# The first pass over two convolution maps at once, row by row

## The chip, the cores and the metric

The kernel runs on one core of a Trainium2 chip. A core has a matrix engine (TensorE, in the profile PE, with its weight loads as PEld), VectorE (DVE), ScalarE (ACT), GpSimd (POOL) and SyncE (SP), each with an instruction queue of its own that runs in order; they wait for one another through semaphores. Weights come from memory by DMA, which SP, ACT and POOL issue. Matmuls write to PSUM, which has eight banks of 512 f32 columns here; everything else stands in SBUF. The metric is the time of one execution on the device in microseconds (us): the median of several runs. Beside it stands one execution with the profiler on.

## The reference

One layer of a decoder trunk for 256 tokens and 16 learned meta tokens in front of them (272 columns in all), width 2048, float32:

```python
u = rms_norm(h, g_pre_mix)
proj = u @ w_in
z_pool, v_conv, g_conv, gate_a, gate_b = split(proj)     # 1024, 1024, 1024, 2048, 2048
y_a = causal_multiscale_pool(z_pool, w_pool_grp, pool_scale) @ w_pool_out
a = v_conv * sigmoid(g_conv)
c = depthwise_causal_conv(a, w_dw) + b_dw                # 31 taps
y_b = silu(layer_norm(c, conv_ln_g, conv_ln_b)) @ w_conv_out
m = sigmoid(gate_a) * y_a + sigmoid(gate_b) * y_b
h = h + rms_norm(m @ w_o, g_post_mix)
f = square(relu(rms_norm(h, g_pre_mlp) @ w_up)) @ w_down
out = (h + rms_norm(f, g_post_mlp))[16:]
```

The change lies in the first lines: the normed input, and the first 256 columns each of `v_conv` and `g_conv`, the two maps whose gated product goes into the convolution.

## The kernel before

**Precision.** Each f32 operand is cut in two parts that the fast matmul type holds: `hi`, a cast on ACT, and `lo`, the rest, a subtraction on DVE. A product of the first projection is three matmuls (`mm3`, L422): weight hi by input hi, weight hi by input lo, weight lo by input hi. Each has 128 weight columns as its stationary side and 272 columns of `u` as its moving side.

**Weights.** `stream` lists all weight chunks of 1 MB in order of use. `open_chunk` (L246) issues a chunk's DMA into one of three `raw` rooms and leaves its casts as pieces to be done; `fetch` opens and splits up to two chunks ahead. A whole chunk is split in one piece: a cast of 128x2048 (L250) and a subtraction of 128x2048 (L253). For the first pass the pieces are rows: one row is 128 input channels, here by 256 columns. The hi and lo parts of chunks rotate through three rooms each.

**The input.** `u` holds, for each of 16 blocks `k` of 128 channels, hi and lo of the input, transposed, with channels on partitions, and times `g_pre_mix`. `x_tile(k)` transposes two blocks of x on TensorE into PSUM (L370); ACT takes the hi part (L371), DVE the lo part (L372). `meta_tokens` does the same for the 16 meta tokens, by 16 transposes of 16 rows. The RMS factor isn't applied to `u`: it depends on the token alone, so it is applied to the products later. `sq_tile` (L380) sums squares on ACT in twelve pieces of 512 columns into `ssq`; `scale_roots` makes the factor and three diagonal tiles from it; `scale_rows` (L412) spreads it over all partitions by f32 matmuls with a tile of ones, and copies it into `rb`. `evac_v` and `evac_g` multiply by `rb`.

**The first passes.** Pass v0 makes 256 columns of `v_conv` in two accumulators. Its loop runs over k with a lead of four: four x tiles and four rows of weights are issued before the first product, then each pair of rows is followed on TensorE by two more x tiles. Pass g0 (256 columns of `g_conv`) and the later ones go through `project`, which takes whole chunks and, after each half chunk, lets `drain` issue some of the `pending` work: the squares, the roots, `after_first` (L412 and the evacuation of v0), `tap_columns`, and then the taps of the convolution. In the profile v0 begins at 7.97 us, g0 at 23.52, and the second pair, v1, at 35.36.

**Before the first product** SP issues the meta tokens and x, ACT `g_pre_mix` and more of x; the framework gives the transfers of SP and ACT eight completion semaphores in turn, so that a ninth one waits for the landing of the first. `keep_warm` (L343) issues transposes of the identity that nobody reads. SP's order is: meta, one half of x's first 512 columns, weight rows, x's third 512 columns, weight rows of the second chunk, x's last columns.

**Later stages** (pool, gates, output projections, the two MLP products, the last norm) aren't touched. A planner orders the last stages by costs and due times; it has no part in what is changed.

Of the kernel before, what the change touches and what calls it, by code (L numbers as in the profile page):

```python
# [8 lines left out]
F32 = mybir.dt.float32  # L9
F32R = mybir.dt.float32r  # L10
AF = mybir.ActivationFunctionType
# [3 lines left out]
P = 128  # L15
CK = 4
CW = 512
# [83 lines left out]
def hybrid_block(ctx: ExitStack, tc: tile.TileContext, ins: dict, out: bass.AP):  # L101
# [83 lines left out]
    G0 = PW + 2 * CC  # L185
    HALF = (2 * CK, CW // 2)
    HALF_CW = CW // 2
    stream = []
# [21 lines left out]
    FIRST = KD // HALF[0]  # L210
    opened = []
    at = {"n": 0, "parts": 0}

# [16 lines left out]
        shift = (place - 1 - 3 * KEYS.index(key)) % 4 * LINE  # L230
        return room[:, shift:shift + CK * CW]

    def open_chunk(first=((2, nc.sync),) * 4):
# [7 lines left out]
        pieces = rows if n < FIRST + 1 else 1  # L241
        k = rows // pieces
        i = 0
        for n_, queue in first if n < FIRST else ((rows, nc.sync),):
            sl = slice(i, i + n_)
            queue.dma_start(raw[:, sl, :], src[:, sl, :])  # L246
            i += n_

        def high(sl):
            nc.scalar.copy(hi[:, sl, :], raw[:, sl, :])  # L250

        def low(sl):
            nc.vector.tensor_sub(lo[:, sl, :], raw[:, sl, :], f32(hi[:, sl, :]))  # L253

        def piece(i):
            def f():
                sl = slice(i * k, (i + 1) * k)
                high(sl)
                low(sl)
            return f  # L260
        opened.append((hi, lo, [piece(i) for i in range(pieces)], flat))

    def split_pieces(c):
        while opened[c][2]:
            opened[c][2].pop(0)()
# [18 lines left out]
    def warm_up(func):  # L284

        nc.scalar.activation(warm, ones[:, 0:1], func)
# [28 lines left out]
    def col(name, k):  # L315
        return vecs[:, cols[name] + k:cols[name] + k + 1]

    def load_x(queue, b, ts=slice(0, NT)):
        sl = slice(b * CW, (b + 1) * CW)
        queue.dma_start(x_in[:, ts, sl], xv[:, ts, sl])  # L320


    nc.sync.dma_start(m_in, meta)
    pre_rows = load_rows(nc.scalar, "g_pre_mix")
    for t, queue in enumerate((nc.sync, nc.scalar)):
        load_x(queue, 0, slice(t, t + 1))
    open_chunk(((1, nc.scalar), (1, nc.sync), (2, nc.sync), (2, nc.sync), (2, nc.sync)))
    load_x(nc.scalar, 1)
# [8 lines left out]
    warm_up(AF.Sqrt)  # L337

    idle = misc_tile("idle")

    def keep_warm(n):
        for _ in range(n):
            nc.tensor.transpose(idle[:, :P], ident, ident)  # L343

    keep_warm(8)

# [1 line left out]

    def meta_tokens():

        pt = acc_tile("xm")[:, :KD * M].rearrange("p (k m) -> p k m", k=KD)
        for k in range(KD):
            nc.tensor.transpose(pt[:, k, :], m_in[:, k * P:(k + 1) * P], ident[:M, :M])
# [4 lines left out]
        nc.scalar.copy(u[:, :, 0, :M], mg)  # L360
        nc.vector.tensor_sub(u[:, :, 1, :M], mg, f32(u[:, :, 0, :M]))

    meta_tokens()
    keep_warm(4)

    def x_tile(k):
        pt = acc_tile(f"xt_{k}")[:, :T]
        sl = slice(k * P, (k + 1) * P)
        for t in range(NT):
            nc.tensor.transpose(pt[:, t * P:(t + 1) * P], x_in[:, t, sl], ident)  # L370
        nc.scalar.activation(u[:, k, 0, M:], pt, AF.Copy, scale=col("g_pre_mix", k))  # L371
        nc.vector.scalar_tensor_tensor(  # L372
            u[:, k, 1, M:], pt, col("g_pre_mix", k), f32(u[:, k, 0, M:]),
            op0=ALU.mult, op1=ALU.subtract)

    def sq_tile(b, t):
        sl = slice(b * CW, (b + 1) * CW)
        junk = tmp.tile([P, CW], F32, tag="junk", bufs=1, name=f"sqx_{b}_{t}")
        src, n = (x_in[:, t, sl], P) if t < NT else (m_in[:, sl], M)
        nc.scalar.activation(junk[:n, :], src, AF.Square, accum_out=ssq[:n, t, b:b + 1])  # L380

    def rsqrt(r, q, var):

# [6 lines left out]
    rb = const.tile([P, L], F32, name="rb")  # L390
    sc = {}

    def scale_roots():
# [23 lines left out]
    def mm3(acc, hi, lo, act, k, cs, first, last):  # L417


        off = act.shape[3] - acc.shape[1]  # L420
        for n, (w, a) in enumerate(((hi, 0), (hi, 1), (lo, 0))):
            nc.tensor.matmul(acc, w[:, k[0], cs], act[:, k[1], a, off:],  # L422
                             start=first and n == 0, stop=last and n == 2)
# [18 lines left out]
    def acc_tiles(name, n=CW // P):  # L442
        return [acc_tile(f"acc_{name}_{j}") for j in range(n)]
# [66 lines left out]


    def pieces_to(n):

        while first["split"] < min(n, (FIRST + 1) * HALF[0]):
            c = first["split"] // HALF[0]
            if c == at["n"]:
                open_chunk()
            opened[c][2].pop(0)()
            first["split"] += 1

    first = {"split": 0}
    accs = [acc[:, :L] for acc in acc_tiles("v0", HALF_CW // P)]
    squares = [(b, t) for b in range(XB) for t in range(NT + 1)]
    LEAD = 4
    for k in range(-LEAD, KD):
        if k < 0:
            x_tile(k + LEAD)

        pieces_to(min(k + LEAD + 1, KD) + 2 * max(k - KD + LEAD + 1, 0))
        if k < 0:  # L530
            continue
        if k >= HALF[0] and k % 2:
            sq_tile(*squares.pop(0))
        for j, acc in enumerate(accs):
            mm3(acc, *opened[k // HALF[0]][:2], u, (k % HALF[0], k), slice(j * P, (j + 1) * P),
                k == 0, k == KD - 1)
        if k % 2:
            for kx in range(k + LEAD - 1, min(k + LEAD + 1, KD)):
                x_tile(kx)
    del opened[:FIRST]  # L540

    def after_first():
        scale_rows()
        for j, acc in enumerate(accs):
            evac_v(j, acc)

    def tap_columns():
# [11 lines left out]
    def first_g(j, acc):  # L559
        pending.append((0, lambda: evac_g(0)(j, acc)))  # L560

    def square_item(s_):
        return (0, lambda: sq_tile(*s_))

    items = [square_item(s_) for s_ in squares]
    pending += items[:4] + [LATER] + items[4:] + [LATER, (0, scale_roots)] + [LATER] * 3
# [1194 lines left out]
```

## Time and profile before

| what | value |
|---|---|
| median of 3 runs | 1207.55 us (1207.3 to 1207.73) |
| profiled execution, own time | 1206.96 us |
| its span, first to last instruction | 1205.2 us |
| TensorE busy | 1195.5 us, 99% |
| DVE busy | 973.5 us, 81% |
| ACT busy | 627.6 us, 52% |
| first product of the first pass | 7.97 us |
| first product of the second pair of passes | 35.36 us |

A line of the timeline has the start, the time, the engine, the line of the kernel, the operation, out<-in by the program's names, shapes, and the count of instructions that it merges; a bracket tells how long the engine stood idle before and what released it. A line of the windows has the stretch, and then for each engine its busy time and number of instructions, the granted clock, the mean share of the DMA engines and GB/s. A line of the DMA view has what was moved, the issuing queue, the count, the size of one and the median time from issue to landing. A line of the groups has a count, and then the sum in us and the mean of one in ns. Matmuls are pipelined: the distance between two starts tells more than the length of one.

### The profile page before, as it was taken

The numbers are of one execution on the slowest core, as the hardware profiler recorded it, in microseconds if no ns is written. First come the engines' busy times: TensorE is split into PE (matmuls) and PEld (weight loads), VectorE is DVE, ScalarE is ACT, GpSimd is POOL, SyncE is SP. The second block draws the span as 40 slices with busy tenths as digits, with TensorE's granted clock in tenths as the row PEclk, the third lists the DMA queues.
The fourth block names the chain that finished last, engine by engine and source line by source line (L and its number), as shares of the span: only waits on it lengthen the run. The fifth ranks groups of instructions, "written<-read, shape, count | busy, mean of one in ns | idle before, by whom it ended". The sixth has DMA issues, their size and how long they took to land.

```text
span 1205.2 us, 15711 instructions
## 1 busy us (share of the span) xinstructions
PE 1195.5 (99%) x6444; PEld 1038.5 (86%) x6444; DVE 973.5 (81%) x1057; ACT 627.6 (52%) x651; POOL 8.3 (1%) x19
## 2 busy tenths in 40 slices
PE   9999999999999999999999999999999999999997
PEld 9999988888888888898888888888888888888886
DVE  6799978999776778678988878778888778788756
ACT  7533344443583455666555564564555555555543
POOL 1000000000000000000000000000000000000000
PEclk9999999999999999999999999999999999999999
DMA  9655565656558578546475564674764754755841
GB/s 289 210 175 176 178 204 179 207 178 207 175 169 279 177 254 266 181 153 229 144 243 175 185 233 158 195 250 140 244 203 153 264 194 156 245 175 172 274 148 70
DMA packets 162038, 238.27 MB, mean 198 GB/s; under 512 B 4033, under 2 KB 91521, under 8 KB 161440
## 3 DMA queue, kind: packets, MB, share of 16 engines
q1 hardware_dynamic: 159120, 229.98, 58.2%
q0 software_dynamic: 1680, 5.40, 1.7%
q10 hardware_dynamic: 1168, 1.91, 0.4%
q8 instruction: 50, 0.82, 0.3%
q14 instruction: 20, 0.16, 0.0%
HBM read 235.17 MB, written 2.10 MB: 197 GB/s over the span
## 4 chain that ended last, share of the span: by engine, by line
PE 99%; DVE 1%; DMA 0%; ACT 0%; DVEq 0%; ACTq 0%; issue 0%
PE bank_u L427 18%; PE acc_gate L682 14%; PE acc_up L1516 14%; PE bank_u L433 9%; PE bank_a L1516 7%; PE o_c L1020 6%; PE bank_b L1516 5%; PE acc_v L422 4%; PE acc_z L422 4%; PE acc_g L422 4%; PE acc_co L682 4%; PE acc_po L682 4%; PE acc_up L427 1%; PE bank_u L1516 1%; PE o_a L1020 1%; PE acc_up L433 1%
## 5 line engine op out<-in xcount | busy, mean ns | idle before, releaser
L427 PE MATMUL bank_u<-m,hi 128*128 128x512 f32 x960 | 329.9, 390 | 0.0
L433 PE MATMUL bank_u<-m,lo 128*128 128x256 f32 x960 | 265.5, 277 | 0.0
L250 ACT CAST hi<-raw 128x2048 fp32r<-128x2048 f32 (+1 forms) x99 | 151.8, 1549 | 189.2 <-PE acc_gate L682 71.5
L1367 DVE TENSOR_TENSOR lo<-raw_m,hi 128x2048 fp32r<-128x2048 f32 x85 | 194.4, 2289 | 59.5 <-ACT hi L1362 59.4
L1362 ACT CAST hi<-raw_m 128x2048 fp32r<-128x2048 f32 x85 | 162.5, 1912 | 138.1 <-PE bank_u L427 76.8
L253 DVE TENSOR_TENSOR lo<-raw,hi 128x2048 fp32r<-128x2048 f32 (+1 forms) x99 | 180.5, 1834 | 44.7 <-ACT hi L250 44.5
L427 PEld LDWEIGHTS bank_u<-m,hi 128*128 128x128 f32 x960 | 180.2, 188 | 38.0
L433 PEld LDWEIGHTS bank_u<-m,lo 128*128 128x128 f32 x960 | 180.4, 188 | 1.6
L682 PE MATMUL acc_gate<-hi,u 128*128 128x512 f32 x512 | 158.4, 390 | 0.0
L1516 PE MATMUL acc_up<-hi,forms 128*128 128x512 f32 x496 | 157.5, 389 | 0.0
L488 DVE SCALAR_TENSOR_TENSOR c<-a,taps,c 128x256 f32<-128x256 f32 x240 | 115.4, 483 | 7.1 <-ACT c L482 0.5
L682 PEld LDWEIGHTS acc_gate<-hi,u 128*128 128x128 f32 x512 | 96.1, 188 | 19.9
L1516 PEld LDWEIGHTS acc_up<-hi,forms 128*128 128x128 f32 x496 | 93.1, 188 | 19.5
L682 PE MATMUL acc_gate<-lo,u 128*128 128x512 f32 x256 | 99.6, 389 | 0.0
L1516 PE MATMUL acc_up<-lo,forms 128*128 128x512 f32 x248 | 96.6, 389 | 0.0
L1367 DVE TENSOR_TENSOR lo<-raw_c,hi 128x2048 fp32r<-128x2048 f32 x29 | 66.4, 2289 | 21.2 <-ACT hi L1362 21.2
L1516 PE MATMUL bank_a<-hi,forms 128*128 128x512 f32 (+1 forms) x256 | 82.0, 383 | 0.0
L1362 ACT CAST hi<-raw_c 128x2048 fp32r<-128x2048 f32 x29 | 55.3, 1908 | 50.9 <-PE bank_u L427 27.9
L1367 DVE TENSOR_TENSOR lo<-raw_a,hi 128x2048 fp32r<-128x2048 f32 x29 | 66.4, 2288 | 17.7 <-ACT hi L1362 17.7
L1362 ACT CAST hi<-raw_a 128x2048 fp32r<-128x2048 f32 x29 | 55.4, 1911 | 42.4 <-PE bank_u L427 19.4
L1020 PE MATMUL o_c<-hi,m 128*128 128x512 f32 x208 | 65.6, 390 | 0.0
L1516 PE MATMUL bank_b<-hi,forms 128*128 128x512 f32 (+1 forms) x200 | 63.7, 382 | 0.0
(310 smaller groups left out, 1856.0 us busy)
## 6 DMA issues: line engine op xcount, KB each, us to landing
raw<-in_w_in_dram SPq DMA_DIRECT2D x54, 1024.0 KB, 5.2
raw_m<-in_w_down_dram SPq DMA_DIRECT2D x37, 1024.0 KB, 5.3
raw_m<-in_w_up_dram SPq DMA_DIRECT2D x33, 1024.0 KB, 6.0
raw_c<-in_w_down_dram SPq DMA_DIRECT2D x14, 1024.0 KB, 5.2
raw_a<-in_w_up_dram SPq DMA_DIRECT2D x13, 1024.0 KB, 5.9
raw_a<-in_w_down_dram SPq DMA_DIRECT2D x13, 1024.0 KB, 5.3
raw_c<-in_w_up_dram SPq DMA_DIRECT2D x12, 1024.0 KB, 6.0
raw_o<-in_w_o_dram SPq DMA_DIRECT2D x10, 1024.0 KB, 7.2
```

Of the source, the lines that this page charges most:

```text
L250: nc.scalar.copy(hi[:, sl, :], raw[:, sl, :])
L253: nc.vector.tensor_sub(lo[:, sl, :], raw[:, sl, :], f32(hi[:, sl, :]))
L422: nc.tensor.matmul(acc, w[:, k[0], cs], act[:, k[1], a, off:], start=first and n == 0, stop=last and n == 2)
L427: nc.tensor.matmul(acc.rearrange("p (a t) -> p a t", a=2)[:, :, ts], hi[:, k[0], cs], act[:, k[1], :, off + ts.start:off + ts.stop], start ...
L433: nc.tensor.matmul(acc[:, :T], lo[:, k[0], cs], act[:, k[1], 0, off:], start=False, stop=stop, skip_group_check=True)
L488: nc.vector.scalar_tensor_tensor(c, conv["a"][:, q, i:i + T], taps[:, q, i:i + 1], c, op0=ALU.mult, op1=ALU.add)
L682: nc.tensor.matmul(acc, act(kk)[:, a_, ts_], w_[:, k, :], start=kk == 0 and n == 0, stop=kk == nk - 1 and n == 2)
L1020: nc.tensor.matmul(acc, form(k, a_), box[w_][:, k, :], start=start and k == 0 and n == 0, stop=stop and k == CK - 1 and n == 2, skip_group ...
L1362: nc.scalar.copy(box["flat"], raw)
L1367: nc.vector.tensor_sub(lo, raw, f32(box["flat"]))
L1516: nc.tensor.matmul(acc, forms[h][:, f, k, a_, :], box[w_][:, k, cs], start=start and k == 0 and n == 0, stop=stop and k == KH - 1 and n == ...
```

## The change

- The first pass makes 256 columns of both maps at once: four accumulators, and a row of weights is 128 channels by 512 columns (256 of each map). So the first four chunks are of four rows, and g0 is no longer a pass of its own.
- Row by row: after the products of row k come the x tiles and the casts of rows some three ahead. The first row is cast in two halves. x tiles go through the two PSUM banks of the other pool, since four accumulators stand in the six of the first.
- Transfers in order of use: x's first 512 columns come as two transfers of 256 columns each for the first two tiles and one for the next; then rows 1 to 3, the next 512 columns of x, four rows, and so on. Each row is one transfer. The meta tokens are loaded twice: early as 256 rows of 128 for two full transposes, and behind all of x as 16 rows for their squares.
- The warm-up runs 7 and later 6 f32 matmuls of ones instead of 8 and 4 transposes. The ones are the first columns of `rb`, set by DVE.
- Squares of x: six pieces of 1024 columns, written over x itself, in rows 6 to 15 of the pass; `scale_roots` stands behind the last row, `after_first`, `tap_columns` and the evacuation of the two g accumulators in the first half of the next pass. The next chunk is split after row 13.
- The hi part of the meta tokens is copied by DVE instead of ACT, its lo part made after the first x tile.

```diff
-    for h in range(CC // HALF_CW):
+    w_vg = w_in[:, PW:PW + 2 * CC].rearrange("(k p) (h c) -> p k h c", p=P, h=2)[:, :, :, :HALF_CW]
+    stream = [(w_vg[:, k:k + CK], (CK, CW)) for k in range(0, KD, CK)]
+    FIRST = len(stream)
+    for h in range(1, CC // HALF_CW):
...
+                for k in range(sl.start, sl.stop):
+                    queue.dma_start(dst[:, k, halves_], src[:, k, halves_])
...
+    rb = const.tile([P, L], F32, name="rb")
+    nc.vector.memset(rb[:, :P], 1.0)
...
+    m_rows = tmp.tile([P, M * KD // P, P], F32, tag="v", bufs=5, name="m_rows")
+    nc.sync.dma_start(m_rows, meta.rearrange("m (k f) -> (m k) f", f=P).rearrange(
+        "(h p) f -> p h f", p=P))
     pre_rows = load_rows(nc.scalar, "g_pre_mix")
+    load_x(nc.sync, 0, slice(0, 1), (0, 1))
+    load_x(nc.scalar, 0, slice(1, 2), (0, 1))
+    open_chunk([(slice(0, 1), slice(0, 1), nc.scalar), (slice(0, 1), slice(1, 2), nc.sync),
+                lambda: load_x(nc.sync, 0, cs=(1, 2)), (slice(1, 4), BOTH, nc.sync)])
+    warm_up(AF.Sqrt)
+    load_x(nc.sync, 1)
+    open_chunk()
     load_x(nc.sync, 2)
     open_chunk()
     load_x(nc.sync, 3)
+    nc.sync.dma_start(m_in, meta)
...
-    ssq = const.tile([P, NT + 1, XB], F32, name="ssq")
+    ssq = const.tile([P, NT + 1, 2], F32, name="ssq")
...
-            nc.tensor.transpose(idle[:, :P], ident, ident)
-    keep_warm(8)
+            nc.tensor.matmul(idle[:, :P], rb[:, :P], rb[:, :P], start=True, stop=True)
+    keep_warm(7)
...
+    accs = [acc[:, :L] for acc in acc_tiles("vg0")]
+    x_tile(0)
+    low_of_meta()
+    row(0)
+    row(0)
+    x_tile(1)
+    row(1)
+    keep_warm(6)
+    for k in range(KD):
+        product_of(k)
+        if k % CK == CK - 1:
+            open_chunk()
+        if k in (0, 2):
+            for kx in (k + 2, k + 3):
+                x_tile(kx)
+                row(kx)
+        elif k % 2 == 0 and k + 3 < KD:
+            x_pair(k + 2)
+        elif k + 3 < KD and k > 1:
+            row(k + 3)
+            row(k + 4)
+        squares = {6: (0, 0), 8: (NT, 0), 10: (1, 0), 12: (NT, 1), 14: (0, 1), 15: (1, 1)}
+        if k in squares:
+            squares_of(*squares[k])
+        if k == 13:
+            split_pieces(FIRST)
     del opened[:FIRST]
+    scale_roots()
...
     pending += [(0, after_first), LATER, (0, tap_columns)]
-    project(u, KD, first_g, "g0", mm=mm3, width=L, fill=2.4)
+    pending += [(0, lambda j=j: evac_g(0)(j, accs[2 + j])) for j in range(2)]
```

More of the change, by code (lines that the diff above doesn't have):

```diff
@@ L231, in part_tile, with open_chunk @@
         return room[:, shift:shift + CK * CW]
-    def open_chunk(first=((2, nc.sync),) * 4):
+    def open_chunk(loads=None):
         n = at["n"]
@@ L240, in open_chunk, with high, low, piece @@
         flat, (raw, hi, lo) = raw, (t.rearrange("p (k c) -> p k c", k=rows) for t in (raw, hi, lo))
-        pieces = rows if n < FIRST + 1 else 1
-        k = rows // pieces
[L243 to L255, printed above, removed]
+        if n < FIRST:
+            dst = raw.rearrange("p k (h c) -> p k h c", h=2)
+            for load in loads or [(slice(i, i + 2), BOTH, nc.sync) for i in range(0, rows, 2)]:
+                if callable(load):
+                    load()
+                    continue
+                sl, halves_, queue = load
+                for k in range(sl.start, sl.stop):
+                    queue.dma_start(dst[:, k, halves_], src[:, k, halves_])
+        else:
+            nc.sync.dma_start(raw, src)
+        pieces = rows if n < FIRST else 1
+        k = rows // pieces
+        def high(sl, cs):
+            nc.scalar.copy(hi[:, sl, cs], raw[:, sl, cs])
+        def low(sl, cs):
+            nc.vector.tensor_sub(lo[:, sl, cs], raw[:, sl, cs], f32(hi[:, sl, cs]))
+        def piece(i, cs):
             def f():
                 sl = slice(i * k, (i + 1) * k)
-                high(sl)
-                low(sl)
-            return f
-        opened.append((hi, lo, [piece(i) for i in range(pieces)], flat))
+                high(sl, cs)
+                low(sl, cs)
+            return f
+        todo = [piece(i, slice(0, width)) for i in range(pieces)]
+        if n == 0:
+            todo[:1] = [piece(0, slice(h * HALF_CW, (h + 1) * HALF_CW)) for h in range(2)]
+        opened.append((hi, lo, todo, flat))
     def split_pieces(c):
@@ L316, in col, with load_x @@
         return vecs[:, cols[name] + k:cols[name] + k + 1]
-    def load_x(queue, b, ts=slice(0, NT)):
-        sl = slice(b * CW, (b + 1) * CW)
+    def load_x(queue, b, ts=slice(0, NT), cs=(0, 2)):
+        sl = slice(b * CW + cs[0] * CW // 2, b * CW + cs[1] * CW // 2)
         queue.dma_start(x_in[:, ts, sl], xv[:, ts, sl])
-    nc.sync.dma_start(m_in, meta)
+    m_rows = tmp.tile([P, M * KD // P, P], F32, tag="v", bufs=5, name="m_rows")
+    nc.sync.dma_start(m_rows, meta.rearrange("m (k f) -> (m k) f", f=P).rearrange(
+        "(h p) f -> p h f", p=P))
     pre_rows = load_rows(nc.scalar, "g_pre_mix")
[L325 to L328, printed above, removed]
+    load_x(nc.sync, 0, slice(0, 1), (0, 1))
+    load_x(nc.scalar, 0, slice(1, 2), (0, 1))
+    BOTH = slice(0, 2)
+    open_chunk([(slice(0, 1), slice(0, 1), nc.scalar), (slice(0, 1), slice(1, 2), nc.sync),
[3 more added lines that the diff above has]
+    open_chunk()
     load_x(nc.sync, 2)
@@ L334, in hybrid_block @@
     nc.gpsimd.dma_start(taps_in, w_dw)
-    ssq = const.tile([P, NT + 1, XB], F32, name="ssq")
+    ssq = const.tile([P, NT + 1, 2], F32, name="ssq")
     nc.gpsimd.memset(ssq, 1.0)
-    warm_up(AF.Sqrt)
-    idle = misc_tile("idle")
+    idle = acc_tile("idle")
     def keep_warm(n):
         for _ in range(n):
-            nc.tensor.transpose(idle[:, :P], ident, ident)
-    keep_warm(8)
+            nc.tensor.matmul(idle[:, :P], rb[:, :P], rb[:, :P], start=True, stop=True)
+    keep_warm(7)
     u = big.tile([P, KD, 2, -(-L // (4 * LINE)) * 4 * LINE], F32R, tag="um", name="u")[:, :, :, :L]
     def meta_tokens():
-        pt = acc_tile("xm")[:, :KD * M].rearrange("p (k m) -> p k m", k=KD)
-        for k in range(KD):
-            nc.tensor.transpose(pt[:, k, :], m_in[:, k * P:(k + 1) * P], ident[:M, :M])
+        pt = acc_tile("xm")[:, :KD * M]
+        for h in range(KD * M // P):
+            nc.tensor.transpose(pt[:, h * P:(h + 1) * P], m_rows[:, h, :], ident)
+        pt = pt.rearrange("p (m k) -> p k m", k=KD)
         rows_to_columns(*pre_rows)
@@ L374, in x_tile, with squares_of @@
             op0=ALU.mult, op1=ALU.subtract)
-    def sq_tile(b, t):
-        sl = slice(b * CW, (b + 1) * CW)
-        junk = tmp.tile([P, CW], F32, tag="junk", bufs=1, name=f"sqx_{b}_{t}")
+    def squares_of(t, b):
+        sl = slice(b * D // 2, (b + 1) * D // 2)
         src, n = (x_in[:, t, sl], P) if t < NT else (m_in[:, sl], M)
-        nc.scalar.activation(junk[:n, :], src, AF.Square, accum_out=ssq[:n, t, b:b + 1])
+        nc.scalar.activation(src, src, AF.Square, accum_out=ssq[:n, t, b:b + 1])
     def rsqrt(r, q, var):
@@ L509, in evac_g, with product_of, row, x_pair @@
         return f
[L512 to L533, printed above, removed]
+    accs = [acc[:, :L] for acc in acc_tiles("vg0")]
+    def product_of(k):
         for j, acc in enumerate(accs):
-            mm3(acc, *opened[k // HALF[0]][:2], u, (k % HALF[0], k), slice(j * P, (j + 1) * P),
+            mm3(acc, *opened[k // CK][:2], u, (k % CK, k), slice(j * P, (j + 1) * P),
                 k == 0, k == KD - 1)
-        if k % 2:
-            for kx in range(k + LEAD - 1, min(k + LEAD + 1, KD)):
-                x_tile(kx)
+    def row(k):
+        opened[k // CK][2].pop(0)()
+    def x_pair(k):
+        x_tile(k)
+        x_tile(k + 1)
+    x_tile(0)
[11 more added lines that the diff above has]
+            for kx in (k + 2, k + 3):
+                x_tile(kx)
+                row(kx)
[9 more added lines that the diff above has]
+            split_pieces(FIRST)
     del opened[:FIRST]
+    scale_roots()
     def after_first():
         scale_rows()
-        for j, acc in enumerate(accs):
+        for j, acc in enumerate(accs[:2]):
             evac_v(j, acc)
```

18 lines of the change are left out of this document (5 added, 13 removed).

## The prediction

> **What bounds the kernel now.** I read the page first: its shares and its chain of what ended last.
>
> ```profile
> span 1205.2 us, 15711 instructions
> PE 1195.5 (99%) x6444; PEld 1038.5 (86%) x6444; DVE 973.5 (81%) x1057; ACT 627.6 (52%) x651; POOL 8.3 (1%) x19
> ...
> PE 99%; DVE 1%; DMA 0%; ACT 0%; DVEq 0%; ACTq 0%; issue 0%
> ```
>
> TensorE is the chain. A change of the first pass can pay only by bringing the same matmuls earlier, so the sum is made at one place: the start of the second pair of passes (L422, acc_v again). The TensorE timeline of the start shows what is lost ahead of it.
>
> ```profile
> 1.36 1.97 PE L343 MATMUL idle<-ident 128*128 128x128 f32 x8 [1.36 <-POOL ident masks.py:199]
> ...
> 6.41 1.91 PE L370 MATMUL xt<-ident,x_in 128*128 128x128 f32 x8
> 7.97 0.80 PE L422 MATMUL acc_v<-u,hi 128*128 128x272 f32 x2
> ...
> 8.85 0.66 PE L422 MATMUL acc_v<-u,hi 128*128 128x272 f32 x2
> 9.30 0.43 PE L422 MATMUL acc_v<-u,lo 128*128 128x272 f32 x1
> 9.53 0.60 PE L422 MATMUL acc_v<-u,hi 128*128 128x272 f32 x2
> 9.97 0.29 PE L422 MATMUL acc_v<-u,lo 128*128 128x272 f32 x1
> ...
> 10.48 0.60 PE L370 MATMUL xt<-ident,x_in 128*128 128x128 f32 x4
> 10.83 0.50 PE L422 MATMUL acc_v<-u,hi 128*128 128x272 f32 x2
> ...
> 12.76 0.50 PE L422 MATMUL acc_v<-u,hi 128*128 128x272 f32 x2
> ...
> 35.36 0.41 PE L422 MATMUL acc_v<-u,hi 128*128 128x272 f32 x2
> ...
> 41.37 1.03 PE L412 MATMUL pb<-diag,ones 16*128 16x16 f32 x6
> ```
>
> The chain, merged, has the pace:
>
> ```profile
> 23.68 11.84 PE acc_g L422 x96
> 35.52 5.92 PE acc_v L422 x48
> ```
>
> A matmul takes 11.84/96 = 0.1233 us, twelve (one row of the new pass) 1.48. From 10.83 to 12.76 lie twelve matmuls and four transposes: 1.93, so four transposes take 0.45. But the five matmuls from 8.85 to 9.97 take 0.224 each: until 9.97 TensorE ran at about half pace. The 192 matmuls (23.68) and the 24 transposes between them (2.70) fill 26.38 of the 27.39 us from 7.97 to 35.36; the missing 1.0 us is this slow stretch. So an undisturbed first product at full pace would have had to start at 8.98 to end at 35.36. That is the figure to beat.
>
> The windows of one microsecond print a clock of 1.00 there (last but two columns), so the spacing of the rows, not that column, shows it:
>
> ```profile
> 1.00:2.00 1.00, 0.64 (x3) 0.65 (x4) 0.00 (x0) 0.00 (x0) 0.96 (x3) 1.00 0.51 131
> ...
> 4.00:5.00 1.00, 1.00 (x12) 1.00 (x11) 0.00 (x0) 0.14 (x1) 0.82 (x3) 1.00 0.85 264
> 5.00:6.00 1.00, 1.00 (x9) 0.96 (x9) 0.36 (x2) 0.00 (x0) 0.00 (x0) 1.00 1.05 357
> 8.00:9.00 1.00, 1.00 (x6) 1.00 (x5) 1.00 (x4) 1.00 (x4) 0.00 (x0) 1.00 1.12 313
> ```
>
> **The change, part by part.**
>
> *Warm-up.* The eight plus four transposes of the identity become seven plus six matmuls of ones. A plain f32 product is two instructions (pb: three products, six instructions in the row above). Eight slow transposes start over 1.91 − 0.42 = 1.49 us, 0.213 apart (6.41; 0.42 is the last one's own length); four fast ones are (0.60 − 0.27)/3 = 0.11 apart. So the seven cost 14 × 0.213 = 3.0 us, from about 1.0 (ones are set by DVE, not behind POOL's identity at 1.36) to 4.0: free, since the columns of x have not landed. The six stand in TensorE's queue between the transposes of x 0 and 1 and the first product, on the path: 12 × 0.11 = 1.3 us at full pace, 12 × 0.213 = 2.6 at half.
>
> *Transfers.* The DMA view of the first 1.5 us, and SP's own waits:
>
> ```profile
> x_in<-in_x_dram SPq DMA_DIRECT2D x1, 256.0 KB, 5.0
> x_in<-in_x_dram ACTq DMA_DIRECT2D x1, 256.0 KB, 5.1
> m_in<-in_meta_dram SPq DMA_DIRECT2D x1, 128.0 KB, 2.8
> rows_g_pre_mix<-in_g_pre_mix_dram ACTq DMA_DIRECT2D x1, 8.0 KB, 3.0
> ...
> 1.18 0.41 SPq L320 DMA_DIRECT2D x_in<-in_x_dram  x1
> ...
> SPq L246 <- DMA rows_g_pre_mix<-in_g_pre_mix_dram: 1.1, 1, 1.1
> ```
>
> x's first columns were issued at 1.18 and landed at 6.2 to 6.3. Now two transfers of 128 KB take their places, same queues and times. They can't land ahead of 1.18 + 3.0 = 4.2 (the 8 KB row's time), nor is there a reason for later than 6.3. To the landing 648 KB were wanted (128 + 8 + 512), now 392. At 6.3 the engines had moved about 1150 KB (windows of one us from 1 to 6 give 131, 103, 176, 264, 357, and 0.3 of the next), so 56% was wanted; the same share puts 392 KB at 700 KB, a little past 5.0. I take 5.2. SP issues more and smaller transfers after that and is held by earlier landings as before (last row); what it moves is in order of use, 384 KB (a row of 256, a tile of 128) for each 1.48 + 0.22 us of TensorE, 226 KB/us against 357 in the row above. So feeding hides, and the meta rows moved behind all of x cost nothing: their squares stand at row 8, some 15 us after the first product.
>
> *ACT and DVE in the pass.* Two windows of 60 us, one per engine, by form:
>
> ```profile
> L250 ACT CAST hi<-raw 128x2048 fp32r<-128x2048 f32 x7 | 13.2, 1901 | 1.9 <-issue 1.9
> L250 ACT CAST hi<-raw 128x256 fp32r<-128x256 f32 x24 | 8.6, 411 | 0.6 <-DMA raw<-in_w_in_dram 0.6
> L371 ACT ACTIVATE u<-xt,vecs 128x256 fp32r<-128x256 f32 x16 | 7.0, 475 | 1.7 <-PE xt L370 1.7
> L380 ACT ACTIVATE sqx<-x_in 128x512 f32<-128x512 f32 x8 | 5.1, 634 | 0.1
> L286 ACT ACT_TABLE_LOAD x2 | 2.6, 1283 | 2.7 <-issue 2.6
> ...
> L253 DVE TENSOR_TENSOR lo<-raw,hi 128x2048 fp32r<-128x2048 f32 x7 | 15.9, 2288 | 9.0 <-ACT hi L250 9.0
> L253 DVE TENSOR_TENSOR lo<-raw,hi 128x256 fp32r<-128x256 f32 x24 | 9.0, 417 | 0.5 <-ACT hi L250 0.5
> L372 DVE SCALAR_TENSOR_TENSOR u<-xt,vecs,u 128x256 fp32r<-128x256 f32 x16 | 7.2, 479 | 2.3 <-ACT u L371 2.3
> ```
>
> A row of 512 costs ACT 0.41 + 256 × (1.901 − 0.411)/1792 = 0.62, DVE 0.68; with the x tile 1.10 and 1.16 of TensorE's 1.70. The pass is TensorE's.
>
> *The first product.* With x at 5.2 and full pace: transposes 0.45, six warm-ups 1.3, start at 6.95. DVE's own chain: ACT's u 5.6 to 6.1, u low 6.6, meta low 7.0 (now on DVE ahead of it), first half row low 7.4; the third matmul wants that at 7.2. So the start counts as 7.15. Then 23.68 + 28 transposes of x (3.15): the pass ends at 33.98 against 35.36, **1.38 us earlier**.
>
> *Squares and norm behind it.* Squares of x become six of 1024 columns, in place. ACT follows its program in order: after row 12, x 14 and 15, the meta square, then the cast of the next chunk. Times from the end of product 12: ACT's x tiles begin 0.51 later (12.82 in the row below, less 12.76 − 0.45 = 12.31, where the twelve ended) and take 0.73, the meta square 0.63 + 0.43 for its second 512 columns, cast 1.90, DVE's low part 2.29: ready at 6.5.
>
> ```profile
> 12.82 0.84 ACT L371 ACTIVATE u<-xt,vecs 128x256 fp32r<-128x256 f32 x2 [0.37 <-PE xt L370]
> 13.55 0.71 ACT L250 CAST hi<-raw 128x256 fp32r<-128x256 f32 x2
> ```
>
> TensorE has 0.45 + 3 × 1.48 = 4.9 us of work and two matmuls on the high part (0.25) before it wants that low part: 5.1. So it **stands 1.3 us**, a wait that before did not have; it gives back what the start won. Two more squares (2.2) then the root, the table load (1.3), five short DVE steps and three diagonals end at about 8.7, and the norm's products come at 6.5 + 22 × 0.123 = 9.2: no wait, but the cover is only 0.5. The next chunk's low part (cast 8.5 to 10.4, low to 12.7) is wanted at about 14. The norm's and taps' matmuls are the same ones, moved from the third and fourth quarter to the first two of the next pass; four accumulators, two evacuated behind the norm, have six banks. Those edits go at nothing.
>
> **The sum**: −1.38 + 1.3 ≈ −0.1 us. The profiled execution took 1206.96 with its span of 1205.2 and would take 1206.9; the median of the runs is 0.6 above it, 1207.55, so the forecast is **1207.4 us**. With x at 4.2 the half row's landing (third in its queue) sets the product at about 6.4: −0.8. With x at 6.3: +1.0. So 1206.7 to 1208.6, within 0.2% (2.4 us), which is about what a measurement of this kernel can tell from no change.
>
> **The rivals.**
>
> *The pace is still half when x lands (ends slower).* What opened it in the trace is told by one fact: transposes ran almost without pause from 1.36 to 7.97 and it stayed shut; it opened 2.0 us after true matmuls began. For the change speaks that its warm-up has 3.0 us of true ones; against it, that they end at 4.0 and more than a microsecond of transposes and waiting follows. If shut, x at 5.2 gives transposes 0.85, six warm-ups 2.6, a start at 8.65, about 0.4 more of slow products: 9.0, so 9.0 − 7.15 = +1.9 on the sum, **1209.3**; with x at 6.3 as well, 1210.3. It decides from the pace at 5.2 alone.
>
> The Trainium skill, page "TensorE: Matmul & The Clock Gate", Part 1, says that TensorE idles at half rate and is let go by a window of some 3.4 us of sustained work, the windows running freely. By this rule 3.0 us of warm-up fill no window by themselves, which speaks for this rival, and executions would differ; by it the sum is +1.9, by the trace's 2.0 us of true matmuls −0.1. Its Part 4 says that transposes don't count as such work; by that rule, the trace agrees (2.0 us after the first product, none of the 6.6 before).
>
> *The stall at the next pass is not there* because ACT or DVE is ahead of my count: the 1.38 is kept, **1206.1**; with x at 4.2, 1205.4.
>
> *The tiles move and the pace of all matmuls with them.* The tile ssq shrinks from 48 to 24 bytes ahead of all large tiles, and the kernel places its operands by lines of 64 bytes; in the layout's steps of 32 everything behind may slide by 32. From the forms below, 512 columns cost 13.60/60 = 0.2267 and 272 cost 0.1233, so a column is 0.43 ns and some 6 to 9 ns of each matmul are something else, which could depend on place. One column's time more or less in 6444 matmuls is 2.8 us: **1210.2 or 1204.6**; it decides the sign from 0.37 ns on. No row of this trace shows two places, so both signs are open; slower is a little likelier since the lines were set for the old place.
>
> ```profile
> 303.42 13.66 PE acc_gate L682 x60
> 317.51 13.62 PE acc_gate L682 x60
> 468.39 13.60 PE o_c L1020 x60
> ```
>
> **How the numbers follow.** Forecast, within about 1.2 us of no change: 0.45. Stall absent: 0.12. Half pace: 0.18, half of it beyond 2.4 us since late transfers come with it. Pace of all matmuls slower 0.14, faster 0.11, both beyond. Faster by 0.2%: 0.11 + 0.03 of the third rival's neighbours (no stall and x early) = 0.14. Slower: 0.09 + 0.14 = 0.23. Within: 0.63. The range runs from no stall with x early to one column more with a little of the half pace, 1205.0 to 1210.6; beyond it lie about 0.1 on each side. The likeliest case alone has 1206.3 to 1208.7.
>
> **What would show it.** The first acc_vg row at 6.9 to 7.4 with 0.123 spacing (half pace: 8.5 or later, 0.22). A gap of 1.0 to 1.6 us two matmuls into the next pass, released by DVE's low part of the first whole chunk. Casts of 128x512 near 0.62, their low parts near 0.68, and no TensorE wait on them or on a DMA between. The norm's products with no wait of their own. 11.84 for 96 matmuls later on: any other figure there is the place of the tiles, and the prediction is wrong by it. It is wrong too if x's half columns land later than 6.3, behind the meta rows that are now 512-byte pieces.

## The result, and the profile after

The changed kernel took **1210.13 us** (median of 13 runs, 1209.22 to 1213.78) beside 1207.73 us for the kernel before (13 runs, 1207.3 to 1209.29): a ratio of 1.0020, with an interval of 1.0012 to 1.0029. It is slower by 2.4 us, just about the 0.2% that was to be told from no change, where 0.1 us less was forecast. The profiled execution took 1210.1 us. Of all executions below one counts as slow, 4994.62 us in the version with all three waits out, and its ratio leaves it out.

The page has the same picture as before, TensorE from end to end, with 3.1 us more of span:

```profile
span 1208.3 us, 15702 instructions
...
PE 1196.3 (99%) x6444; PEld 1039.1 (86%) x6444; DVE 974.6 (81%) x1051; ACT 625.4 (52%) x630; POOL 8.3 (1%) x19
...
PE 98%; DVE 1%; ACT 1%; issue 0%; DVEq 0%; ACTq 0%
```

So the place to read is again TensorE's timeline of the start (columns: start, length, engine, line, operation, count, and in brackets idle time with what ended it). The rows answer to those shown of before:

```profile
1.05 3.35 PE L366 MATMUL idle<-rb 128*128 128x128 f32 x14 [1.05 <-DVE rb L291]
...
4.80 0.77 PE L396 MATMUL xt<-ident,x_in 128*128 128x128 f32 x4
...
6.67 0.50 PE L447 MATMUL acc_vg<-u,hi 128*128 128x272 f32 x2
...
7.22 0.41 PE L447 MATMUL acc_vg<-u,hi 128*128 128x272 f32 x2
...
7.59 0.41 PE L447 MATMUL acc_vg<-u,hi 128*128 128x272 f32 x2
...
33.93 0.41 PE L447 MATMUL acc_v<-u,hi 128*128 128x272 f32 x2
35.51 0.39 PE L447 MATMUL acc_v<-u,lo 128*128 128x272 f32 x1 [1.17 <-DVE lo L262]
35.74 0.41 PE L447 MATMUL acc_v<-u,hi 128*128 128x272 f32 x2
...
38.42 1.03 PE L437 MATMUL pb<-diag,ones 16*128 16x16 f32 x6
...
42.36 0.26 PE L326 MATMUL pv_pool_scale<-ident,rows_pool_scale 48*128 48x48 f32 x1
44.20 0.68 PE L589 MATMUL taps_t<-ident,taps_in 31*128 31x31 f32 x8 [1.58 <-DVE rb L439]
...
45.86 0.65 PE L447 MATMUL acc_v<-u,hi 128*128 128x272 f32 x2
...
46.54 0.65 PE L447 MATMUL acc_v<-u,hi 128*128 128x272 f32 x2
...
111.60 0.41 PE L447 MATMUL acc_z<-u,hi 128*128 128x272 f32 x2
```

The same view of the kernel before, at the rows that were not shown yet:

```profile
45.30 0.26 PE L312 MATMUL pv_pool_scale<-ident,rows_pool_scale 48*128 48x48 f32 x1
45.49 0.68 PE L551 MATMUL taps_t<-ident,taps_in 31*128 31x31 f32 x8
...
108.37 0.41 PE L422 MATMUL acc_z<-u,hi 128*128 128x272 f32 x2
```

Up to 33.93 the change does what was predicted. The second pair of passes began at 35.36 before: **1.43 us won**. What follows gives back more than that, at three places:

- At 35.51 a matmul on a low part has waited for DVE. Its two forerunners on the high part began at 33.93, so at 0.1233 each it could have begun at 34.18: **1.33 lost**. The next matmul follows it after 0.23 us instead of 0.12 (35.51 to 35.74), another **0.11**.
- From the row of `pv_pool_scale` to `taps_t` lie 1.84 us (42.36 to 44.20) where 0.19 lay before (45.30 to 45.49): **1.65 lost**. This wait was not predicted.
- From 45.86 to 46.54 three matmuls take 0.68 us, 0.227 each instead of 0.1233: about half pace. The windows of this stretch (start and end, length, then busy time and count of TensorE, its weight loads, DVE, ACT and GpSimd, granted clock, DMA share and GB/s) show how long:

```profile
42.40:44.20 1.80, 0.22 (x2) 0.10 (x1) 1.77 (x3) 1.80 (x1) 0.00 (x0) 1.00 0.70 213
45.40:48.80 3.40, 3.40 (x17) 3.40 (x16) 3.40 (x6) 0.83 (x2) 0.00 (x0) 0.50 1.10 351
48.80:52.00 3.20, 3.20 (x27) 3.20 (x27) 2.01 (x5) 0.60 (x1) 0.00 (x0) 1.00 0.84 273
```

From 45.4 to 48.8 the granted clock is 0.50 and only 17 matmuls fall into the window (those that cross its edges counted too), against 27 in the 3.2 us behind it. By the starts of the single matmuls the stretch runs from 45.41 to 48.82, 3.41 us, in which 15 follow one another; at full pace 15 take 1.85, so **1.56 is lost**. It was not predicted either.

The sum is −1.43 + 1.44 + 1.65 + 1.56 = +3.22. At the first product of `acc_z`, behind all the passes of the maps, the two kernels stand 111.60 − 108.37 = 3.23 apart, so nothing else of weight happened. The chain agrees that the pace of the passes themselves is untouched, 11.84 for 96 matmuls as before:

```profile
52.56 11.84 PE acc_g L447 x96
```

The medians differ by 2.4 and not by 3.1: the profiled execution of the changed kernel lies at its median (1210.1 beside 1210.13), while that of the kernel before lies 0.77 below its own (1206.96 beside 1207.73); why it does isn't shown. The half-pace stretch isn't in every execution, by the mean granted clock of each. Half a clock for 3.41 us of 1208 is 0.0014 of it. Of the thirteen, the seven with a mean of 0.996 took 1210.1 us or more, the three with 0.998 or 0.999 took 1209.2 to 1209.6, and the three with 0.997 lie on both sides (1209.4 to 1210.7). So the stretch probably comes in most executions, not in all.

**Why `taps_t` waits.** TensorE's waits name the engine and line:

```profile
PE taps_t L589 <- DVE rb L439: 1.6, 1, 1.6
```

L439 copies the norm from `pb` to `rb`. `taps_t` is the second tile asked for behind `pb` from a pool of two PSUM banks, so it gets the bank of `pb`, and that is free only when the copy has read it. DVE's timeline of the changed kernel shows when that was:

```profile
33.16 2.29 DVE L262 TENSOR_TENSOR lo<-raw,hi 128x2048 fp32r<-128x2048 f32 x1 [2.31 <-ACT hi L259]
...
37.00 0.62 DVE L431 TENSOR_SCALAR diag<-ident,r_in 128x128 f32<-128x128 f32 x3
39.30 4.49 DVE L262 TENSOR_TENSOR lo<-raw,hi 128x2048 fp32r<-128x2048 f32 x2 [1.69 <-ACT hi L259]
43.72 0.43 DVE L439 COPY rb<-pb 128x272 f32<-128x272 f32 x1
```

and that of the kernel before:

```profile
40.39 0.61 DVE L406 TENSOR_SCALAR diag<-ident,r_in 128x128 f32<-128x128 f32 x3
42.69 2.29 DVE L253 TENSOR_TENSOR lo<-raw,hi 128x2048 fp32r<-128x2048 f32 x1 [1.69 <-ACT hi L250]
44.90 0.43 DVE L414 COPY rb<-pb 128x272 f32<-128x272 f32 x1
```

Before, one low part of 2.29 us stood between the diagonals and the copy; now two stand there. The norm's products moved 2.95 us ahead (41.37 to 38.42) and the taps' transposes would have (45.30 to 42.36 for the row in front of them), but the copy between them moved only 1.18 (44.90 to 43.72). And there had been next to no cover before: the copy ended at 45.33, 0.16 us ahead of `taps_t`.

### The profile page after: what moved, and what is told of

It reads as the page before. It is cut to its first block, busy times and chain, and to the rows that moved or that the text cites. A ratio compares the mean times of both kernels' runs of the same rounds, so it can differ in the third digit from the quotient of the medians.

```text
span 1208.3 us, 15702 instructions
## 1 busy us (share of the span) xinstructions
PE 1196.3 (99%) x6444; PEld 1039.1 (86%) x6444; DVE 974.6 (81%) x1051; ACT 625.4 (52%) x630; POOL 8.3 (1%) x19
## 4 chain that ended last, share of the span: by engine, by line
PE 98%; DVE 1%; ACT 1%; issue 0%; DVEq 0%; ACTq 0%
PE bank_u L452 18%; PE acc_gate L712 14%; PE acc_up L1546 14%; PE bank_u L458 9%; PE bank_a L1546 7%; PE o_c L1050 6%; PE bank_b L1546 5%; PE acc_z L447 4%; PE acc_co L712 4%; PE acc_po L712 4%; PE acc_g L447 3%; PE acc_v L447 3%; PE acc_vg L447 2%; PE acc_up L452 1%; PE bank_u L1546 1%; PE o_a L1050 1%
## 5 line engine op out<-in xcount | busy, mean ns | idle before, releaser
L259 ACT CAST hi<-raw 128x2048 fp32r<-128x2048 f32 (+2 forms) x91 | 150.8, 1666 | 196.9 <-PE acc_gate L712 67.7
L262 DVE TENSOR_TENSOR lo<-raw,hi 128x2048 fp32r<-128x2048 f32 (+2 forms) x91 | 179.9, 1984 | 47.5 <-ACT hi L259 47.0
```

The lines of the kernel that those rows point to most:

```text
L259: nc.scalar.copy(hi[:, sl, cs], raw[:, sl, cs])
L262: nc.vector.tensor_sub(lo[:, sl, cs], raw[:, sl, cs], f32(hi[:, sl, cs]))
```

## The experiments

The theory to be tested: the change itself lands where it was forecast, and the loss is the wait of the taps' transposes on the copy of `rb`, with a half-pace stretch that this hole brings on. The rivals: the loss lies elsewhere, or the half pace has nothing to do with the hole. Later runs ask what the waits are worth together and what the warm-up is worth. All edits are to the changed kernel. Three medians of the kernel before belong to them: 1207.73 (with the changed kernel), 1207.57 (with the first four experiments) and 1207.45 (with the last four); each ratio is to its own, and can differ from the quotient of the medians by some 0.0002.

### The taps a quarter later

```diff
-    pending += [(0, after_first), LATER, (0, tap_columns)]
+    pending += [(0, after_first), LATER, LATER, (0, tap_columns)]
```

> One half chunk more stands between the norm's products and the transposes of the taps; nothing else is changed. Theory (the taps' bank is still held by the copy into rb, which DVE does behind two low parts of whole chunks, 1.65 us, and the half pace of 3.4 us afterwards comes from this hole): the wait of 1.6 us at taps_t goes, the pace stays at 0.123 us from the first pass on, and the time falls by 1.65 + 1.7 to about 1206.8 us. Rival (the half pace comes from the first stall, at DVE's low part, or from the start): the wait goes but the slow stretch stays, about 1208.5. Rival (the tap columns are wanted early, so the convolution pays): no gain, 1210.

Measured: **1207.66 us**, ratio 1.0000 (0.9991 to 1.0009). The wait is gone from TensorE's waits, and so is the half pace, in the same windows as above:

```profile
42.40:44.20 1.80, 1.80 (x16) 1.80 (x16) 1.76 (x3) 1.80 (x1) 0.00 (x0) 1.00 0.79 221
45.40:48.80 3.40, 3.40 (x31) 3.31 (x32) 3.25 (x7) 0.43 (x1) 0.00 (x0) 1.00 1.09 352
```

TensorE is busy for all of both windows at a clock of 1.00. The granted clock agrees over all eleven executions: each has a mean of 0.998 or 0.999. One marker in a list takes off the whole loss, and what is left is the forecast sum: 1.4 won at the start, 1.3 given back at the low part. The time was 0.9 above the theory's figure and 0.8 below the rival's, so by itself it does not choose between them; the profile does, since behind the warm-up no TensorE wait of weight is left but the predicted one, and no half pace.

### The hole filled with products into the bank at hand

```diff
...
+            for _ in range(7):
+                nc.tensor.matmul(pv[:, P:2 * P], ones, ones, start=True, stop=True)
```

The seven products stand behind the transpose into `pv` and ahead of `taps_t`; nothing reads them.

> Seven f32 products of ones that nobody reads (14 passes, about 1.55 us) are put between the transpose of the row vectors and the transposes of the taps, where TensorE waits anyway. Theory (the half pace is TensorE's answer to a stretch almost without true matmuls): the taps still begin at the same time, 44.2, but the pace stays at 0.123 us and the time falls by about 1.7 us to 1208.4. Rival (the half pace has another cause): no change, 1210.

Measured: **1212.86 us**, ratio 1.0045 (1.0032 to 1.0058). The edit failed, and TensorE's timeline says why:

```profile
34.81 0.41 PE L447 MATMUL acc_v<-u,hi 128*128 128x272 f32 x2
...
43.24 0.26 PE L588 MATMUL pv_pool_scale<-ident,rows_pool_scale 48*128 48x48 f32 x1
46.03 1.83 PE L591 MATMUL pv_pool_scale<-ones 128*128 128x128 f32 x14 [2.52 <-DVE vecs L589]
47.78 0.68 PE L594 MATMUL taps_t<-ident,taps_in 31*128 31x31 f32 x8
```

The fillers write the tile that DVE is to copy out (`vecs`), so they waited for that copy, which stands on DVE behind the copy of `rb` and two products with it. The hole became 2.5 us instead of 1.6, and 1.8 us of fillers came behind it. It says nothing of the clock as it was meant to, but it shows once more that whatever waits for DVE here waits behind both low parts. The hole of this execution was not followed by half pace. Others of its five may have had the stretch: the two with a mean granted clock of 0.998 took 1212.2 us, those with 0.996 and 0.995 took 1213.9 and 1214.6. The row of 34.81 also tells something of the start, which is the changed kernel's own up to there: the second pair of passes began 0.88 us later than in the changed kernel's profile. Its warm-up was at half pace for longer: the four transposes of x from 4.98 take 0.91 us (0.61 in the changed kernel) and the twelve passes behind them 1.73 (1.26).

### The first whole chunk split by rows

```diff
-        pieces = rows if n < FIRST else 1
+        pieces = rows if n < FIRST + 1 else 1
```

> The first whole chunk is split in eight rows again, as the kernel before does, instead of in one piece. Theory (behind the first stall stands the chain of squares, root, diagonals and copy, which is late in itself): the stall of 1.3 us at DVE's low part goes, but ACT's casts take 1.0 us longer, so TensorE now waits for the diagonals at the norm's products, 1.6 us, and at the taps 2.7 instead of 1.65; the time is 1210 to 1211.5. Rival (the stall is a cost of its own): the time falls by 1.3 us to 1208.8.

Measured: **1211.34 us**, ratio 1.0030 (1.0018 to 1.0042), within the theory's range. The stall at the low part is gone, but the time is not won. TensorE's waits:

```profile
PE taps_t L589 <- DVE rb L439: 2.3, 1, 2.3
PE pb L437 <- DVE diag L431: 1.3, 1, 1.3
```

Now the norm's own products wait 1.3 us for the diagonals. This is the step that the prediction called covered by only 0.5 us: the stall at the low part was itself the cover. With TensorE ahead by 1.3, the chain of squares, root and diagonals ends last. The wait of the taps is longer, and half pace follows again, in this kernel's own window:

```profile
46.30:49.70 3.40, 3.40 (x17) 3.40 (x17) 3.40 (x6) 0.83 (x2) 0.00 (x0) 0.50 1.10 351
```

### All three waits out

```diff
-        pieces = rows if n < FIRST else 1
+        pieces = rows if n < FIRST else 2 if n == FIRST else 1
...
-    pending += [(0, after_first), LATER, (0, tap_columns)]
+    pending += [LATER, (0, after_first), LATER, LATER, (0, tap_columns)]
```

The first whole chunk comes in two pieces, the norm's products come a quarter of a pass later, and the taps two quarters later.

> The first whole chunk is split in two pieces, the norm's products come one half chunk later, and the taps two more. Theory (the start is 1.4 us better, and all of the loss lies in the waits behind it and the slow stretch that they cause): no TensorE wait between the first product and 60 us, full pace throughout, 1.3 + 1.65 + 1.7 less than the changed kernel: 1205.5 to 1206.3 us, faster than both. Rival (the four-accumulator pass, the place of the tiles or the transfers cost something too): 1207.5 or more without any such wait.

Measured: **1206.71 us**, ratio 0.9992 (0.9983 to 1.0001): a little above what was expected. The profiled execution, of 1207.06 us, had the late opening too: its second pair of passes began at 34.74. One wait is left behind the warm-up, for the low part of the second whole chunk, whose cast stands on ACT behind the norm's squares, root and table load:

```profile
PE acc_v L447 <- DVE lo L262: 0.5, 1, 0.5
```

### The hole filled with products that wait for nothing

```diff
...
+        for _ in range(7):
+            nc.tensor.matmul(spare["acc"][:, 3 * P:], ones, ones, start=False, stop=True,
+                             skip_group_check=True)
```

`spare["acc"]` is the accumulator in use, written in its last 128 columns, which nobody reads.

> The changed kernel, with the seven f32 products of ones written to unused columns of an accumulator that nobody reads then, between the transpose of the row vectors and those of the taps; in the earlier try they went to the bank of that transpose and waited for its copy themselves. Theory (half pace answers a stretch almost without true matmuls): TensorE is fed through the wait, the taps begin as late as in the changed kernel (1.85 us behind the row vectors), but no stretch at half pace follows in any execution, so the executions lie as low as the fastest of the changed kernel, 1209.0 to 1209.6. Rival (another cause): half pace follows as before, 1210 and more.

Measured: **1209.07 us**, ratio 1.0012 (1.0003 to 1.0021), within the theory's range and outside the rival's. TensorE's timeline:

```profile
42.29 0.26 PE L326 MATMUL pv_pool_scale<-ident,rows_pool_scale 48*128 48x48 f32 x1
42.48 1.83 PE L592 MATMUL acc_v<-ones 128*128 128x128 f32 x14
44.23 0.68 PE L596 MATMUL taps_t<-ident,taps_in 31*128 31x31 f32 x8
...
45.32 0.41 PE L447 MATMUL acc_v<-u,hi 128*128 128x272 f32 x2
...
45.70 0.41 PE L447 MATMUL acc_v<-u,hi 128*128 128x272 f32 x2
```

The transposes start at 44.23, as late as in the changed kernel: the fillers take up the time of the wait, so that TensorE is not idle in it. The products behind it keep 0.41 us for two, and all eleven executions have a mean granted clock of 0.998 or 0.999, against 0.996 or 0.997 in ten of the changed kernel's thirteen. This separates the two terms: by the ratios, the half pace is worth 1.0020 − 1.0012 = 0.0008, 1.0 us (less than the 1.56 of the profile; not every execution has it), and the wait 1.0012 − 1.0000 = 0.0012, 1.4 us. The intervals of these ratios are about as wide as the terms, so the profiles carry the split. The half pace follows from TensorE standing without products, not from what DVE does at that time, which is the same here.

### Every wait out, second try

```diff
-        pieces = rows if n < FIRST else 1
+        pieces = rows if n < FIRST else 2 if n < FIRST + 2 else 1
...
-    pending += [(0, after_first), LATER, (0, tap_columns)]
+    pending += [LATER, (0, after_first), LATER, LATER, (0, tap_columns)]
```

> As the version with all waits out, and the second whole chunk is split in two pieces as well, since its low part was the one wait left (0.5 us released by DVE's low part at 41.8). Theory: no TensorE wait of 0.3 us or more between the first product and 60 us, 0.5 to 0.6 us less than that version: 1206.1. Rival: the wait goes to another step (the copy into rb, the taps) and the time stays at 1206.7.

Measured: **1205.97 us** (1205.59 to 1206.38), ratio 0.9986 (0.9977 to 0.9995). This version beats both kernels, by 1.5 us the one before and, by the ratios, by some 4 the changed one. TensorE's waits have one row left, the wait for the first constants:

```profile
PE idle L366 <- DVE rb L291: 1.1, 1, 1.1
```

Its timeline, for the two runs that follow:

```profile
6.85 0.49 PE L447 MATMUL acc_vg<-u,hi 128*128 128x272 f32 x2
...
34.23 0.41 PE L447 MATMUL acc_v<-u,hi 128*128 128x272 f32 x2
```

### Three products of warm-up instead of six, on the path

On top of the version without waits:

```diff
-    keep_warm(6)
+    keep_warm(3)
```

> As the version without waits, with three instead of six warm-up products between the x tiles and the first product. Theory (they stand on the path and cost 12 passes): six passes less give 0.65 us at full pace, but the first product then waits for DVE's low part of the half row, so 0.2 to 0.4 us less: 1205.8. Rival (the six keep the pace): the gate opens later, the first products are slow, 1206.5 or more.

Measured: **1206.08 us**, ratio 0.9988 (0.9980 to 0.9997), no different from the version with six. TensorE's timeline:

```profile
5.95 0.39 PE L447 MATMUL acc_vg<-u,hi 128*128 128x272 f32 x1
...
6.49 0.39 PE L447 MATMUL acc_vg<-u,hi 128*128 128x272 f32 x1 [0.15 <-DVE u L390]
...
34.21 0.41 PE L447 MATMUL acc_v<-u,hi 128*128 128x272 f32 x2
```

The first product starts 0.9 us sooner (0.4 of it is the x tiles, at 4.58 instead of 4.98), but then waits in small pieces for DVE, and the second pair of passes begins at 34.21 instead of 34.23. So the six products cost next to nothing here. DVE's chain of u, the meta columns and the first low half row sets the pace at first, as the prediction had it; then row 1 does, whose weights landed late: its cast begins on ACT at 7.88, after 1.31 us of waiting for the DMA, and TensorE's matmul on its low part only at 9.29.

### Transposes for warm-up again

On top of the version without waits:

```diff
-            nc.tensor.matmul(idle[:, :P], rb[:, :P], rb[:, :P], start=True, stop=True)
+            nc.tensor.transpose(idle[:, :P], ident, ident)
```

> As the version without waits, with transposes of the identity in place of the f32 products in both warm-ups, as in the kernel before. Theory (transposes don't open the pace): full pace comes about 2 us after the first product, which costs 1.0 us of the products and the transposes between; the second warm-up is one pass instead of two each, which gives 0.6 back: 1206.5 to 1207. Rival (transposes open it as well): 1205.5, faster than with products, since the second warm-up is shorter.

Measured: **1206.17 us**, ratio 0.9991 (0.9982 to 1.0000), between the two expectations. TensorE's timeline:

```profile
4.58 1.12 PE L396 MATMUL xt<-ident,x_in 128*128 128x128 f32 x4 [0.67 <-DMA x_in<-in_x_dram]
...
6.63 0.80 PE L447 MATMUL acc_vg<-u,hi 128*128 128x272 f32 x2
...
8.14 0.66 PE L447 MATMUL acc_vg<-u,hi 128*128 128x272 f32 x2
...
9.24 0.28 PE L447 MATMUL acc_vg<-u,lo 128*128 128x272 f32 x1
...
34.96 0.41 PE L447 MATMUL acc_v<-u,hi 128*128 128x272 f32 x2
```

The products start at half pace (0.66 for two) and get the full one from about 9.2, 2.6 us after the first. The second pair begins at 34.96 instead of 34.23. So products instead of transposes are worth 0.7 us between these two profiles, and 0.2 in the medians, which is not to be told from nothing. The second pair began at 34.74 and 34.81 in two profiles with products, so most of the 0.7 can be the execution. The rows also show when x's half columns had landed: at 4.58.

## Why the prediction was wrong

**The figure to beat, and what the start gains: right.** The pass was to end at 33.98, 1.38 us ahead; it ended at 33.93, 1.43 ahead. Two errors cancelled, and a third thing was luck (next paragraph). x's half columns landed earlier than the 5.2 that I took from the share of bytes. The DMA view of the changed kernel (last number: us from issue to landing):

```profile
x_in<-in_x_dram ACTq DMA_DIRECT2D x1, 128.0 KB, 3.5
x_in<-in_x_dram SPq DMA_DIRECT2D x1, 128.0 KB, 3.3
```

They took 3.3 and 3.5 us against 5.0 and 5.1 of the whole columns, so TensorE met them at 4.80 straight from its own work, and the first product came at 6.67 instead of 6.95 to 7.15. Against that, from 6.67 to 33.93 lie 27.26 us where 26.83 of products and transposes were counted: 0.43 in small gaps.

**The pace at the first product: right, but when it opens is luck.** It was full there: the twelve passes of the warm-up ahead of it took 1.26 us (5.41 to 6.67), and the rows of 7.22 and 7.59 are three matmuls apart, 0.37. The rival of half pace at the first product did not come, in this execution or in those of the experiments that kept the products. Half pace did last into the second warm-up in some: of the four profiles with the same instructions up to the second pair of passes, three reach it at 33.93, 33.92 and 33.85 and the one with the late fillers at 34.81, which is a gain of 0.55 and not of 1.43. **The place of the tiles: no effect**, 11.84 for 96 both times.

**The stall at the low part: right**, 1.3 predicted, 1.33 measured (1.44 with the slow step behind it), at the matmul named. That the norm's products would not wait was right too, and the third experiment shows that this hung on the stall ahead of them.

**The step that failed** is the last of the second part: "The norm's and taps' matmuls are the same ones, moved from the third and fourth quarter to the first two of the next pass ... Those edits go at nothing." They are the same matmuls and cost the same themselves. What went wrong is that the copy of `rb`, which frees the bank that the taps need, is on DVE and did not move with them: a second low part of 2.29 us now stands ahead of it. This gave +1.65 for the wait, and with it +1.56 for the half pace behind, neither of which is in the sum. The step named six banks for the accumulators and never asked who frees the other two. The row that would have told it stands in the trace of before: the copy ended 0.16 us ahead of the transposes that needed its bank. I had named the cover of the norm's products (0.5 us) and not that of the work behind them. That 1210.13 still lies inside the stated 1205.0 to 1210.6 is luck: its upper end stood for a slower pace of all matmuls with a little half pace at the start, and the pace of all matmuls did not change.

The second half of the miss, the half pace, had no row in the trace of before, where no such hole occurs behind the start. That the first half was the cause of the second is shown by the two runs that took away one of them at a time: with the taps later both are gone, with the hole filled only the second.

The same rule of the clock that the prediction weighed for the start bears on this place. The Trainium skill, page "TensorE: Matmul & The Clock Gate", Part 1, says that an idle window of about 3.4 us brings the half rate back, that windows run freely, and, in Part 4, that transposes don't count as work. The stretch of 3.41 us at 0.50 agrees with a window of that length, and the executions without it agree with windows that run freely. The hole here was shorter, though: 2.5 us from the last full-pace product before 42.36 to the next at 44.81, with a few transposes in it. The measurement decides: in this execution a hole of 2.5 us was enough.

## What to carry to other kernels

When a step is moved ahead on one engine, list who must free each buffer that it takes, and see whether that release moves too: a release on another engine, queued behind work that stays where it is, turns into a wait, and the slack to compare with is a row of the trace of before. Cover counts down the whole chain: a wait that goes uncovers the next late step (here the diagonals behind the low part, then the second low part), so a start that is earlier by 1.4 us paid only when the three waits behind it were taken out together. On TensorE a hole can cost about twice its length (here 1.65 us and 1.56 behind it), since half pace may follow it; filling it with products that wait for nothing is a way to tell the two apart.

## What the runs showed of the hardware

- A hole of 2.5 us with only a few transposes in it was followed by 3.41 us at a granted clock of 0.50, in the changed kernel (hole 42.36 to 44.81, half pace 45.41 to 48.82). In the one with the chunk by rows a hole of 3.2 us (42.60 to 45.76) was followed by 3.4 us of it (46.3 to 49.7). In the profiled execution of the one with the late fillers a hole of 2.8 us (43.24 to 46.03) was followed by none. The loss is 1.56 us in the changed kernel's profile.
- The full pace at the start opened 2.6 us after the first product when only transposes stood ahead of it (at about 9.2), but ahead of the first product where plain products had run from 1.05 on. The time at which it opened differed between executions of the same start, by 0.9 us at the second pair of passes (33.93 and 34.81). In the median, products instead of transposes were worth 0.2 us, which is not to be told from nothing.
- With two transfers of 128 KB in place of two of 256 KB at the start, and other transfers around them changed too, the time to their landing went from 5.0 and 5.1 to 3.3 and 3.5 us: a larger gain than the share of all bytes had led me to expect, and still far from half.
